# Adding up half of the first unit's modulation on TensorE in the opening of a hybrid attention and pooling block

## The chip, the cores and the metric

The kernel runs on one core of a Trainium2 chip. The metric is the device time of one execution in microseconds (us); the kernel before took 1557.66 us, the median of three runs.

## The reference

One decoder layer over 256 tokens of width 4096, all in f32, with a conditioning vector c of length 4096. Cut to what matters here:

```python
c_act = jax.nn.silu(c)
mod = c_act @ w_ada[l] + b_ada[l]                 # (1,4096) @ (4096, 12288)
shift, scale, gate = jnp.split(mod, 3, axis=-1)
h = rmsnorm(x, norm_gain[l])
h = h * (1.0 + scale[:, None, :]) + shift[:, None, :]
proj = jnp.einsum('bsd,dn->bsn', h, w_in[l])      # (256,4096) @ (4096,12288)
...                                               # attention, pooling, gating give y
y = y @ w_out[l]
x = x + gate[:, None, :] * y
return rmsnorm(x, final_gain)
```

The large product needs h, h needs shift and scale, and these are a vector times a 4096 x 8192 matrix, which has to be read from memory first.

## The kernel before, in words

**Units.** The 4096 rows of h are handled in 16 units of 256 rows, two blocks of 128 each. Unit u needs columns 256u to 256u+255 of the shift part and of the scale part of w_ada, 512 columns over all 32 row blocks. `ada_tasks` (line 174) makes 16 tasks for a unit. Each fetches two row blocks, here called a pair, into one `raw` tile of 512 KB by two transfers (line 193), and hands the adding up to `late_work`, which holds it back by one task. So the first unit has pairs 0 to 15. The adding up, `ada_acc` (line 153), is one VectorE instruction for each row block: the accumulator plus the block times its column of `cact` (silu of c, spread over the 128 partitions). For the first unit the accumulator is the SBUF tile `aflat`, for later ones a PSUM tile.

**build_h** (line 201) closes a unit: TensorE transposes the accumulator in four pieces (line 210), VectorE sums over the 128 rows (line 212, `pc`), three small VectorE operations make shift and scale columns (lines 216 to 218), ScalarE applies them to the transposed x (line 226, `hf`) and rounds (line 228, `hh`), and VectorE takes the remainder (line 229, `hl`).

**The opening.** All 16 tasks of the first unit are issued before anything else, `A0 = 1` unit, with the column constants (line 131) put in after the fourth task and the eight loads of x after the fifth. ScalarE squares x with a running sum (line 325), lines 147 to 151 make the reciprocal root, VectorE makes two diagonal tiles `diag_r` from it (line 330), and TensorE multiplies x by them in f32 (line 338), which transposes and scales it: here called the flips, in sixteen groups of four, of which twelve stand ahead of the first unit's transposes and four behind. ScalarE copies each group out (line 342).

**The visits.** After that the kernel goes over 24 chunks of 512 columns of w_in again and again, each time with the units that are ready. A piece of w_in (two row blocks by 512 columns) is fetched into a `raw` tile (line 236), rounded on ScalarE (`wh`, line 242), its remainder taken on VectorE (`wl`, line 243), and multiplied in three products on TensorE (line 253). The adding up of the next unit runs beside it at a fixed rate.

**What sets the order.** Each engine works off its instructions in the order in which the built program has them. All transfers are issued on SP in order. There are seven `raw` tiles in turn, for pairs of w_ada and pieces of w_in alike, so each transfer into one waits until the tile seven places earlier has been read. Four PSUM tiles `psm` serve flips, transposes and later accumulators.

```python
RAWB = 7
...
    todo.insert(EARLY, load_columns)
...
                for q in range(NFLIP):
                    flip_x(q)
    for u in range(A0):
        build_h(u, first[u][0][0], hp, xT)
    for q in range(NFLIP, 8):
        flip_x(q)
```

Of the kernel before, what the change touches and what calls it, by code (L numbers as in the profile page):

```python
# [7 lines left out]
F32 = mybir.dt.float32  # L8
F32R = mybir.dt.float32r
AF = mybir.ActivationFunctionType  # L10
ALU = mybir.AluOpType
AX = mybir.AxisListType

P = 128
S = 256
NT = S // P
D = 4096
KT = D // P
CH = 512
# [11 lines left out]
A0 = 1  # L31
# [24 lines left out]
def tile_hybrid_block(  # L56
# [17 lines left out]
    nc = tc.nc  # L74
# [4 lines left out]
    strm = ctx.enter_context(tc.tile_pool(name="strm", bufs=2))  # L79
# [8 lines left out]
    ps_m = ctx.enter_context(tc.tile_pool(name="ps_m", bufs=PSMB, space=PSUM))  # L88

    def misc():  # L90
        return ps_m.tile([P, CH], F32, name="psm")

    def raw_tile():
        return strm.tile([P, RAW], F32, name="raw", bufs=RAWB)
# [11 lines left out]
    cact = const.tile([P, KT], F32, name="cact")  # L106
# [46 lines left out]
    def ada_acc(acc, rt, kts, width, init=None):  # L153
        for i, kt in enumerate(kts):
            r = rt[:, i * width:(i + 1) * width]
            if kt == 0 and init is None:
                nc.vector.tensor_scalar(out=acc, in0=r, scalar1=cact[:, 0:1], scalar2=None, op0=ALU.mult)
            else:
                nc.vector.scalar_tensor_tensor(out=acc, in0=r, scalar=cact[:, kt:kt + 1],  # L159
                                               in1=init if kt == 0 else acc,  # L160
                                               op0=ALU.mult, op1=ALU.add)
# [3 lines left out]
    def late_work(f, lag=None):  # L165
        delayed.append(f)
        while len(delayed) > (HOLD if lag is None else lag):
            delayed.pop(0)()

    def flush_work():  # L170
        while delayed:
            delayed.pop(0)()

    def ada_tasks(u, pool):
        w = 2 * UNITS[u] * P
        n = RAW // w
        cs = slice(US[u] * P, US[u + 1] * P)
        acc = []
        tasks = []
        for a in range(0, KT, n):  # L180
            kts = list(range(a, min(KT, a + n)))

            def f(kts=kts):
                if not acc:
                    acc.append((adap.tile([P, 2 * HB * P], F32, name="aflat") if u < A0 else misc())[:, 0:w])
                rt = raw_tile()
                m = len(kts)
                v = rt[:, 0:m * w].rearrange("p (n s d) -> p n s d", n=m, s=2)
                if m == 1:
                    nc.sync.dma_start(out=v[:, 0], in_=wa_v[:, kts[0], 0:2, cs])  # L190
                else:
                    for i in range(2):
                        nc.sync.dma_start(out=v[:, :, i], in_=wa_v[:, kts[0]:kts[-1] + 1, i, cs])
                late_work(lambda: ada_acc(acc[0], rt, kts, w))
            tasks.append(f)
        return acc, tasks

# [3 lines left out]
    def build_h(u, acc, pool, xT):  # L201
        flush_work()
        uk, k0 = UNITS[u], US[u]
        if u >= A0:
            flat = adap.tile([P, 2 * HB * P], F32, name="aflat")
            nc.scalar.copy(out=flat[:, 0:2 * uk * P], in_=acc)
            acc = flat
        pt = misc()
        for j in range(2 * uk):
            nc.tensor.transpose(out=pt[:, j * P:(j + 1) * P], in_=acc[:, j * P:(j + 1) * P], identity=ident)  # L210
        pc = const.tile([P, 2 * HB], F32, name="pc", bufs=2)
        nc.vector.tensor_reduce(out=pc[:, 0:2 * uk], in_=pt[:, 0:2 * uk * P].rearrange("p (j d) -> p j d", d=P),
                                axis=AX.X, op=ALU.add)
        s12 = const.tile([P, 2, HB], F32, name="s12", bufs=2)
        ks = slice(k0, k0 + uk)
        nc.vector.tensor_tensor(out=s12[:, 0, 0:uk], in0=pc[:, 0:uk], in1=colB[:, ks], op=ALU.add)
        nc.vector.tensor_tensor(out=s12[:, 1, 0:uk], in0=pc[:, uk:2 * uk], in1=gainc[:, ks], op=ALU.mult)
        nc.vector.tensor_tensor(out=s12[:, 1, 0:uk], in0=s12[:, 1, 0:uk], in1=gb[:, ks], op=ALU.add)  # L218
        for a in range(0, uk, 2):
            kk = k0 + a  # L220
            if kk % HB == 0:
                htile[kk // HB] = [pool.tile([P, HB, S], F32R, name=n, align_bytes=LINE) for n in ("hh", "hl")]
            hh, hl = [v[:, kk % HB:kk % HB + 2] for v in htile[kk // HB]]
            hf = strm.tile([P, 2, S], F32, name="hf")
            for i in range(2):
                nc.scalar.activation(out=hf[:, i], in_=xT[:, kk + i], func=AF.Identity,  # L226
                                     scale=s12[:, 1, a + i:a + i + 1], bias=s12[:, 0, a + i:a + i + 1])
            nc.scalar.copy(out=hh, in_=hf)
            nc.vector.tensor_tensor(out=hl, in0=hf, in1=hh.bitcast(F32), op=ALU.subtract)  # L229
            for i in range(2):  # L230
                hs[kk + i] = (hh[:, i], hl[:, i])
# [81 lines left out]
    done = [0] * NCH  # L313
    used = [0] * NCH
    first = [ada_tasks(u, adap) for u in range(A0)]
    todo = [f for _, t in first for f in t]
    xs = []
# [36 lines left out]
# [5 lines that stand above are left out]
    state = {"ready": A0, "built": A0, "cur": ada_tasks(A0, adap), "credit": 0.0, "age": 0}  # L359

    def ada_hook(n):
        st = state
        st["credit"] += n * RATES[min(st["built"], len(RATES) - 1)]
        st["age"] += 1
        while st["cur"] and st["cur"][1] and st["credit"] > 0:
            if len(st["cur"][1]) == 1 and min(used) < ((US[st["built"] + 1] - 1) // HB - WIN + 1) * HB:
                st["credit"] = 0.0
                break
            st["cur"][1].pop(0)()
            st["credit"] -= ADA_COST  # L370
        if st["cur"] and not st["cur"][1]:
            u = st["built"]
            build_h(u, st["cur"][0][0], hp, xT)
            st["built"] += 1
            st["age"] = 0
            st["cur"] = ada_tasks(u + 1, adap) if u + 1 < NU else None
        if st["age"] >= LAG:
            st["ready"] = st["built"]
# [219 lines left out]
    for c, ch in enumerate(order):  # L598
# [5 lines left out]
        elif 12 <= ch < 16:  # L604
            i = ch - 12
# [145 lines left out]
```

## Time and profile before

| | |
|---|---|
| three runs | 1555.61, 1557.66, 1560.14 us; median 1557.66 |
| the profiled execution | 1554.48 us, of which span 1552.7 us |
| TensorE (PE) | 1504.9 us busy, 97% of the span |
| VectorE (DVE) | 1393.0 us, 90% |
| ScalarE (ACT) | 822.9 us, 53% |
| GpSimd (POOL) | 384.3 us, 25% |
| transfers | 491.15 MB, mean 316 GB/s |

The span is the time from the first to the last instruction of the execution that the profiler took; 1.78 us lie around it. A busy share says how long an engine had something in work, not that it set the pace. All times in rows are us from the start of the span unless marked ns.

### The profile page before, as it was taken

To read this page: it belongs to the slowest core of one execution; us is meant where nothing else is said; L and a number is where in the kernel's file an instruction comes from. 1 tells how busy PE (TensorE), PEld (TensorE's weight loads), DVE (VectorE), ACT (ScalarE), POOL (GpSimd) and SP (SyncE) were. 2 spreads that over 40 slices of the span, in tenths; PEclk is the share of its full clock that TensorE was granted. 3 is DMA by queue.
4 is the path that set the end of the run, shared out by engine and by line. 5 is a ranking of instruction groups with operands and counts; after the bars stand their busy time and mean duration, and the time that the engine had idled before them with its cause. 6 is when DMAs were issued, how large, how long until landed. Compare 5 with 4: busy or idle time off the path is not lost.

```text
span 1552.7 us, 20698 instructions
## 1 busy us (share of the span) xinstructions
PE 1504.9 (97%) x6979; PEld 1247.7 (80%) x6979; DVE 1393.0 (90%) x1666; ACT 822.9 (53%) x1075; POOL 384.3 (25%) x235
## 2 busy tenths in 40 slices
PE   3999999999999999999999999999999999999997
PEld 2777788888888888888888888888898878888875
DVE  5999999999989889898899998999988889888886
ACT  5666555555555655555555554556554434444434
POOL 0001545555454545545453431000000000000000
PEclk9999999999999999999999999999999999999999
DMA  9999999999999899999999999886777999999986
GB/s 334 356 355 369 313 332 309 346 299 348 332 300 347 297 342 307 321 350 324 330 349 309 335 344 327 286 268 208 247 240 259 307 346 346 340 330 324 325 307 245
DMA packets 324091, 491.15 MB, mean 316 GB/s; under 512 B 19320, under 2 KB 150664, under 8 KB 323984
## 3 DMA queue, kind: packets, MB, share of 16 engines
q1 hardware_dynamic: 323984, 489.82, 92.8%
q8 instruction: 55, 0.90, 0.2%
q14 instruction: 52, 0.43, 0.1%
HBM read 485.55 MB, written 4.19 MB: 315 GB/s over the span
## 4 chain that ended last, share of the span: by engine, by line
PE 88%; DMA 5%; DVE 4%; issue 1%; ACT 1%; SPq 0%; DVEq 0%; ACTq 0%
PE mm L253 82%; DMA raw<-in_w_ada_dram 3%; DVE wl L243 1%; DVE aflat L159 1%; PE psm L628 1%; PE psm L253 1%; DVE gacc L159 1%; DMA raw<-in_w_out_dram 1%; DMA sb<-in_x_dram 0%; PE psm L210 0%; PE psm L421 0%; PE psm L445 0%; DMA raw<-in_w_in_dram 0%; PE psm L534 0%; PE psm L533 0%
## 5 line engine op out<-in xcount | busy, mean ns | idle before, releaser
L242 ACT CAST wh<-raw 128x1024 fp32r<-128x1024 f32 x514 | 537.5, 1051 | 546.1 <-PE mm L253 408.1
L243 DVE TENSOR_TENSOR wl<-raw,wh 128x1024 fp32r<-128x1024 f32 x514 | 715.0, 1396 | 56.7 <-ACT wh L242 53.5
L253 PE MATMUL mm<-wh,hh 128*128 128x512 f32 x1536 | 603.8, 393 | 4.1 <-ACT wh L242 3.3
L253 PE MATMUL mm<-wh,hl 128*128 128x512 f32 x1536 | 599.8, 391 | 0.2 <-DVE hl L229 0.2
L253 PE MATMUL mm<-wl,hh 128*128 128x512 f32 x1536 | 414.8, 391 | 0.0
L159 DVE SCALAR_TENSOR_TENSOR psm<-raw,cact,psm 128x512 f32<-128x512 f32 x465 | 349.3, 751 | 18.5 <-DMA raw<-in_w_ada_dram 11.9
L299 POOL TENSOR_TENSOR sa<-part,sa 128x512 f32<-128x512 f32 x150 | 250.3, 1690 | 410.7 <-ACT part L298 410.7
L253 PEld LDWEIGHTS mm<-wh,hh 128*128 128x128 f32 x1536 | 288.5, 188 | 65.9 <-ACT wh L242 6.7
L253 PEld LDWEIGHTS mm<-wl,hh 128*128 128x128 f32 x1536 | 287.2, 188 | 61.0 <-DVE wl L243 1.8
L253 PEld LDWEIGHTS mm<-wh,hl 128*128 128x128 f32 x1536 | 288.6, 188 | 58.8 <-DVE hl L229 0.5
L253 PE MATMUL mm<-wh,sa 128*128 128x512 f32 x896 | 221.6, 389 | 0.0
L159 DVE SCALAR_TENSOR_TENSOR gacc<-raw,cact,gacc 128x512 f32<-128x512 f32 x248 | 185.8, 749 | 23.7 <-DMA raw<-in_w_ada_dram 19.5
L253 PEld LDWEIGHTS mm<-wh,sa 128*128 128x128 f32 x896 | 168.0, 188 | 34.8
L299 POOL TENSOR_TENSOR sb<-part,sb 128x512 f32<-128x512 f32 x80 | 133.2, 1687 | 151.9 <-ACT part L298 151.9
L298 ACT COPY part<-mm 128x512 f32<-128x512 f32 x230 | 124.0, 589 | 29.7 <-PE mm L253 29.7
L253 PE MATMUL mm<-wl,sa 128*128 128x512 f32 x448 | 120.0, 390 | 1.3 <-DVE wl L243 1.2
L253 PEld LDWEIGHTS mm<-wl,sa 128*128 128x128 f32 x448 | 83.9, 188 | 19.5 <-DVE wl L243 2.1
L338 PE MATMUL psm<-diag_r,sb 128*128 128x128 f32 x128 | 16.2, 292 | 15.9 <-DMA raw<-in_w_ada_dram 15.9
L159 DVE SCALAR_TENSOR_TENSOR aflat<-raw,cact,aflat 128x512 f32<-128x512 f32 x31 | 23.3, 752 | 8.4 <-DMA raw<-in_w_ada_dram 7.5
L338 PEld LDWEIGHTS psm<-diag_r,sb 128*128 128x128 f32 x128 | 16.0, 208 | 16.0 <-DVE diag_r L330 16.0
L294 ACT COPY sa<-mm 128x1024 f32<-128x1024 f32 x16 | 16.3, 1017 | 13.1 <-PE mm L253 13.0
L226 ACT ACTIVATE hf<-xT,s 128x256 f32<-128x256 f32 x32 | 17.5, 596 | 10.3 <-DVE s L218 10.3
(124 smaller groups left out, 709.4 us busy)
## 6 DMA issues: line engine op xcount, KB each, us to landing
raw<-in_w_in_dram SPq DMA_DIRECT2D x384, 512.0 KB, 5.7
raw<-in_w_ada_dram SPq DMA_DIRECT2D x512, 256.0 KB, 5.4
raw<-in_w_ada_dram SPq DMA_DIRECT2D x128, 512.0 KB, 5.9
raw<-in_w_out_dram SPq DMA_DIRECT2D x128, 512.0 KB, 6.3
sb<-in_x_dram SPq DMA_DIRECT2D x16, 512.0 KB, 5.7
raw<-in_w_pool_dram SPq DMA_DIRECT2D x8, 512.0 KB, 4.3
out_dram<-sb SPq DMA_DIRECT2D x16, 256.0 KB, 2.6
fg<-in_final_gain_dram SPq DMA_DIRECT2D x8, 256.0 KB, 4.8
```

The source lines that it names most:

```text
L159: nc.vector.scalar_tensor_tensor(out=acc, in0=r, scalar=cact[:, kt:kt + 1], in1=init if kt == 0 else acc, op0=ALU.mult, op1=ALU.add)
L226: nc.scalar.activation(out=hf[:, i], in_=xT[:, kk + i], func=AF.Identity, scale=s12[:, 1, a + i:a + i + 1], bias=s12[:, 0, a + i:a + i + 1])
L242: nc.scalar.copy(out=wh[:, 0:n], in_=v[:, 0:n])
L243: nc.vector.tensor_tensor(out=wl[:, 0:n], in0=v[:, 0:n], in1=wh[:, 0:n].bitcast(F32), op=ALU.subtract)
L253: nc.tensor.matmul(pt[t], lhsT=hv[i][p][:, t * P:(t + 1) * P], rhs=w[:, i], start=started, stop=ended)
L294: nc.scalar.copy(out=accs[ch], in_=pt)
L298: nc.scalar.copy(out=part, in_=pt[:, t])
L299: nc.gpsimd.tensor_tensor(out=accs[ch][:, t], in0=part, in1=accs[ch][:, t], op=ALU.add)
L338: nc.tensor.matmul(px[:, i * S + t * P:i * S + (t + 1) * P], lhsT=xs[q][:, t, (2 * a + i) * P:(2 * a + i + 1) * P], rhs=diag_r[:, t], star ...
L628: nc.tensor.matmul(pt[t], lhsT=h[:, t * P:(t + 1) * P], rhs=w, start=False, stop=last and e == len(seq) - 1)
```

## The change

For the first unit alone, the even row block of each pair is added up on VectorE as before, and the odd one by a TensorE matmul with one column of `cact` as stationary tile and the 512 columns of the block as moving data, into one row of a PSUM tile `row` that is kept over the whole opening. build_h copies that row to SBUF on ScalarE and adds it on VectorE to the first row of `aflat`, ahead of the transposes.

```diff
+    row = ps_m.tile([P, CH], F32, name="psm")
+
+    def row_acc(rt, kts, width):
+        for i, kt in enumerate(kts):
+            r = rt[:, i * width:(i + 1) * width]
+            if kt % 2 == 0:
+                ada_acc(first[0][0][0], rt, kts[:1], width)
+            else:
+                nc.tensor.matmul(row[0:1, 0:width], lhsT=cact[:, kt:kt + 1], rhs=r, start=(kt == 1), stop=(kt == KT - 1))
...
-                late_work(lambda: ada_acc(acc[0], rt, kts, w))
+                if u < A0:
+                    late_work(lambda: row_acc(rt, kts, w))
+                else:
+                    late_work(lambda: ada_acc(acc[0], rt, kts, w))
...
+        if u < A0:
+            line = strm.tile([P, 2, S], F32, name="hf").rearrange("p a s -> p (a s)")
+            nc.scalar.copy(out=line[0:1], in_=row[0:1])
+            nc.vector.tensor_tensor(out=acc[0:1], in0=acc[0:1], in1=line[0:1], op=ALU.add)
```

Lines after these stand 10 to 17 lines lower in the changed kernel (the flips at 355, the matmuls of the visits at 270, the row matmuls at 182).

On TensorE, the end of the twelfth flip group and the first unit's transposes, before:

```order
L338 MATMUL psm<-diag_r,sb 128x128 [waits DMAHW4_49,Activation_49]
L338 MATMUL psm<-diag_r,sb 128x128 x3
L338 MATMUL psm<-diag_r,sb 128x128 [waits Activation_49]
L338 MATMUL psm<-diag_r,sb 128x128 x3
L210 MATMUL psm<-ident,aflat 128x128 [waits DVE_49,Activation_49]
L210 MATMUL psm<-ident,aflat 128x128 x3
```

The same place now, where lines 355 and 227 are the flips and the transposes:

```order
L355 MATMUL psm<-diag_r,sb 128x128 [waits Activation_49]
L355 MATMUL psm<-diag_r,sb 128x128 x3
L182 MATMUL psm<-raw,cact 1x512 [waits DMAHW4_49,DMAHW3_49]
L182 MATMUL psm<-raw,cact 1x512 [waits DMAHW6_49,DMAHW5_49]
L182 MATMUL psm<-raw,cact 1x512 [waits DMAHW7_49,DMAHW0_49]
L182 MATMUL psm<-raw,cact 1x512 [waits DMAHW2_49,DMAHW1_49]
L182 MATMUL psm<-raw,cact 1x512 [waits DMAHW4_49,DMAHW3_49]
L182 MATMUL psm<-raw,cact 1x512 [waits DMAHW6_49,DMAHW5_49]
L182 MATMUL psm<-raw,cact 1x512 [waits DMAHW7_49,DMAHW0_49]
L182 MATMUL psm<-raw,cact 1x512 [waits DMAHW2_49,DMAHW1_49]
L182 MATMUL psm<-raw,cact 1x512 [waits DMAHW4_49,DMAHW3_49]
L227 MATMUL psm<-ident,aflat 128x128 [waits DVE_49]
```

Of the 16 row matmuls, those of pairs 0 to 6 stand ahead of the flips and the nine of pairs 7 to 15 between the twelve flip groups and the transposes.

On SP, the transfers of pairs 13 (`raw_299`), 14 (`raw_304`) and 15 (`raw_309`), of the first piece of w_in (`raw_362`), of the next unit's first two pairs and of the second piece of w_in, now:

```order
L203 DMA raw_299<-in_w_ada_dram 128x2x256 [waits DMAHW7_49,DVE_49,PE_49]
L203 DMA raw_299<-in_w_ada_dram 128x2x256 [waits DMAHW0_49]
L203 DMA raw_304<-in_w_ada_dram 128x2x256 [waits DMAHW1_49,DVE_49,PE_49]
L203 DMA raw_304<-in_w_ada_dram 128x2x256 [waits DMAHW2_49]
L203 DMA raw_309<-in_w_ada_dram 128x2x256 [waits DMAHW3_49,DVE_49,PE_49]
L203 DMA raw_309<-in_w_ada_dram 128x2x256 [waits DMAHW4_49]
L253 DMA raw_362<-in_w_in_dram 128x2x512 [waits DMAHW5_49,DVE_49,PE_49]
L203 DMA raw_381<-in_w_ada_dram 128x2x256 [waits DMAHW6_49,DVE_49,PE_49]
L203 DMA raw_381<-in_w_ada_dram 128x2x256 [waits DMAHW7_49]
L203 DMA raw_384<-in_w_ada_dram 128x2x256 [waits DMAHW0_49,DVE_49,PE_49]
L203 DMA raw_384<-in_w_ada_dram 128x2x256 [waits DMAHW1_49]
L253 DMA raw_392<-in_w_in_dram 128x2x512 [waits DMAHW2_49,DVE_49,PE_49]
```

The order of the transfers is the same as before; what is new is the wait for TensorE beside the one for VectorE. Pair 14 takes the tile of pair 7, pair 15 that of pair 8, and the first piece of w_in that of pair 9.

On ScalarE, from the twelve flip copies to the rounding of h, now (259 is the rounding of a w_in piece, 223 the copy of the row, 243 and 245 make `hf` and `hh`):

```order
L359 COPY xT<-psm 128x512 [waits PE_49] x12
L259 CAST wh<-raw 128x1024 [waits DMAHW5_49]
L223 COPY hf<-psm 1x512 [waits PE_49,Activation_49]
L359 COPY xT<-psm 128x512 [waits PE_49]
L243 ACTIVATE hf<-xT,s_326 128x256 [waits DVE_49,Activation_49]
L243 ACTIVATE hf<-xT,s_326 128x256
L359 COPY xT<-psm 128x512 [waits PE_49]
L245 CAST hh<-hf 128x512 [waits Activation_49]
```

The new copy of the row stands behind the rounding of the first w_in piece. VectorE has its instructions in the like order: the remainder of that piece, then the add of the row, then the sum over the transposes. From the second unit on, the order of all engines is that of before but for a few early places of ScalarE and VectorE.

## Rows read from the trace of the kernel before

**Rows 1.** The page, chain that ended last, share by engine.

```profile
PE 88%; DMA 5%; DVE 4%; issue 1%; ACT 1%; SPq 0%; DVEq 0%; ACTq 0%
```

**Rows 2.** Busy time by stage: PE, PEld, DVE, ACT, POOL, granted clock, DMA share, GB/s.

```profile
300.00:600.00 300.00, 300.00 (x1335) 248.39 (x1334) 275.68 (x282) 170.31 (x222) 156.53 (x93) 1.00 0.96 321
```

**Rows 3.** Timeline of VectorE, opening: start, length, operation, count, idle before and releaser.

```profile
9.48 3.20 DVE L159 SCALAR_TENSOR_TENSOR aflat<-raw,cact,aflat 128x512 f32<-128x512 f32 x4 [0.24 <-DMA raw<-in_w_ada_dram]
...
24.70 2.33 DVE L159 SCALAR_TENSOR_TENSOR aflat<-raw,cact,aflat 128x512 f32<-128x512 f32 x3
...
27.07 0.75 DVE L159 SCALAR_TENSOR_TENSOR aflat<-raw,cact,aflat 128x512 f32<-128x512 f32 x1
27.73 0.48 DVE L330 TENSOR_SCALAR diag_r<-ident,rr 128x128 f32<-128x128 f32 x2
28.13 14.13 DVE L159 SCALAR_TENSOR_TENSOR aflat<-raw,cact,aflat 128x512 f32<-128x512 f32 x18
...
43.68 1.22 DVE L243 TENSOR_TENSOR wl<-raw,wh 128x1024 fp32r<-128x1024 f32 x1
```

**Rows 4.** Timeline of TensorE, opening.

```profile
11.49 0.42 PE L137 MATMUL psm<-ident,rows 112*128 112x112 f32 x1 [7.92 <-DMA rows<-in_pool_scale_dram]
...
28.07 12.50 PE L338 MATMUL psm<-diag_r,sb 128*128 128x128 f32 x96 [15.86 <-DMA raw<-in_w_ada_dram]
42.41 0.63 PE L210 MATMUL psm<-ident,aflat 128*128 128x128 f32 x4 [1.84 <-DVE aflat L159]
42.87 3.74 PE L338 MATMUL psm<-diag_r,sb 128*128 128x128 f32 x32
47.47 0.50 PE L253 MATMUL mm<-wh,hh 128*128 128x512 f32 x1 [0.87 <-ACT hh L228]
```

**Rows 5.** Timeline of ScalarE, opening.

```profile
12.49 0.63 ACT L325 ACTIVATE hf<-sb 128x512 f32<-128x512 f32 x1 [0.29 <-DMA sb<-in_x_dram]
...
20.48 0.63 ACT L325 ACTIVATE hf<-sb 128x512 f32<-128x512 f32 x1 [1.33 <-DMA sb<-in_x_dram]
...
32.56 0.59 ACT L342 COPY xT<-psm 128x512 f32<-128x512 f32 x1 [0.31 <-PE psm L338]
...
41.09 1.05 ACT L242 CAST wh<-raw 128x1024 fp32r<-128x1024 f32 x1
```

**Rows 6.** Timeline of the SP queue: issues of transfers in the opening.

```profile
1.65 4.01 SPq L193 DMA_DIRECT2D raw<-in_w_ada_dram  x8
...
15.19 18.70 SPq L193 DMA_DIRECT2D raw<-in_w_ada_dram  x22
34.32 0.37 SPq L236 DMA_DIRECT2D raw<-in_w_in_dram  x1
```

**Rows 7.** The page, DMA issues: count, size, median us from issue to landing.

```profile
raw<-in_w_in_dram SPq DMA_DIRECT2D x384, 512.0 KB, 5.7
```

**Rows 8.** Groups by line and shape: count, busy us, mean ns, idle before.

```profile
L342 ACT COPY xT<-psm 128x512 f32<-128x512 f32 x16 | 9.4, 586 | 10.4 <-PE psm L338 10.4
L229 DVE TENSOR_TENSOR hl<-hf,hh 128x512 fp32r<-128x512 f32 x16 | 11.8, 739 | 1.8 <-ACT hh L228 1.8
```

**Rows 9.** The chain in order of time: the first long run of the visits.

```profile
48.20 30.01 PE mm L253 x131
```

**Rows 10.** Busy time by stage, with the granted clock third from the end.

```profile
28.00:30.00 2.00, 1.93 (x9) 1.93 (x10) 1.93 (x5) 0.00 (x0) 0.00 (x0) 1.00 1.10 351
...
1542.00:1546.00 4.00, 0.00 (x0) 0.00 (x0) 2.84 (x9) 2.13 (x5) 0.00 (x0) 1.00 1.04 399
1546.00:1547.00 1.00, 0.00 (x0) 0.00 (x0) 1.00 (x3) 0.74 (x2) 0.00 (x0) 0.89 0.88 338
```

**Rows 11.** Waits of TensorE from 47 to 145 us: total, times, longest.

```profile
PE mm L253 <- ACT wh L242: 3.3, 4, 2.0
```

**Rows 12.** Timeline of ScalarE at 78 us, where the longest of these waits lies.

```profile
78.23 1.01 ACT L294 COPY sb<-mm 128x1024 f32<-128x1024 f32 x1 [1.70 <-PE mm L253]
79.14 2.00 ACT L242 CAST wh<-raw 128x1024 fp32r<-128x1024 f32 x2
```

## The prediction

> **What bounds the kernel now.** I read the chain that ended last first: 88% of it is TensorE [rows 1], and between 300 and 600 us TensorE is busy without a gap [rows 2]. Once the visits run, the end is their start plus a fixed amount of matmul work, so a change in the opening counts by what it does to the first visit matmul, at 47.47 us [rows 4], after which 131 matmuls follow without a break from 48.20 on [rows 9]. Next I read the opening engine by engine. Its last stretch belongs to VectorE: 18 row blocks in one piece from 28.13 to 42.26 [rows 3], then TensorE's transposes at 42.41, after 1.84 us of waiting for `aflat` [rows 4]. TensorE itself has the flips from 28.07 to 40.57 and four flip groups more behind the transposes, 3.74 us [rows 4]. SP is well ahead: the transfers of pairs 5 to 15, 22 of them, are all issued by 33.89 and the first piece of w_in at 34.32 [rows 6].
>
> **The change part by part, from the span's start.**
>
> VectorE loses 16 row blocks at 0.75 us, 12 us of work. That is worth something only if the sum is then complete earlier, and the order says that it is not: nine of the 16 row matmuls stand on TensorE behind the twelve flip groups.
>
> Start and end of the flips. They wait for `diag_r`. Before, VectorE did three row blocks from 24.70 (2.33 us), the reciprocal, one more row block, and then `diag_r` at 27.73 [rows 3]. Now it does two row blocks there and none after the reciprocal: about 1.2 us less, so the flips start at about 26.9 instead of 28.07. A flip group costs 0.59 of copy plus 0.31 of ScalarE waiting for TensorE, 0.90 us [rows 5]; twelve make 10.8, but they took 12.5, so 1.7 us are a slow start after a long idle stretch [rows 4]. Now the row matmuls of pairs 4 to 6 run just ahead of them and may take that slow start away, or not: end at 37.7 or 39.4. Nothing tells which; I take the middle, 38.5, against 40.57 before.
>
> The row matmuls. The rows have no f32 matmul with 512 columns and one stationary column. The nearest is a flip group, f32 as well, four times 128 columns: 0.90 us. A visit matmul, 512 columns in the rounded type, follows the last one after 0.23 us (131 in 30.01) [rows 9], which is the lower end; twice 0.90, as in the slow start, is the upper. I take 0.9, since type and column count are the same. Nine behind the flips make 8.1 us: 38.5 to 46.6 if their data are there.
>
> The early seven cost nothing if ScalarE's squares cover them. Those of pairs 0 to 3 push the transposes of line 137, at 11.49 before [rows 4], back by about 1.4 us at the slow rate (pair 3 was used from about 11.0 on, two blocks after 9.48 [rows 3], plus 1.8). The squares, which began at 12.49, then begin near 13.8. They had 1.33 us of waiting for x before 20.48 [rows 5], which takes it up; without that cover it would be 1.3 us more. The `row` tile holds one of four PSUM tiles, so the flips turn over in three; ScalarE is 0.31 us ahead in each group, so that costs nothing either.
>
> The transfers. This is the part that hangs on SP. Pair 14 needs the `raw` tile of pair 7, which TensorE now reads after the flips, at 38.5 + 0.9 = 39.4. So SP stops behind pair 13, and queued behind it are pairs 14 and 15, the first w_in piece and the next unit's pairs. Pair 14 goes out at 39.4, pair 15 at 40.3, w_in at 41.2, where before it went out at 34.32. When does that piece land? By the median from issue to landing, 5.7 us [rows 7], at 46.9. By the start of the program, the other place where the queue starts empty: first issue at 1.65 [rows 6], third tile used at 9.48 as it landed [rows 3], 7.8 us later, so 47.2. By bandwidth alone, three tiles of 0.52 MB at 351 GB/s [rows 10], 4.5 us, at 43.9: the lower end. I take 47.1.
>
> From there to the transposes. ScalarE rounds the piece, 1.05 [rows 5], to 48.2. Only then, in its order, comes the copy of `row`, 0.59 like a flip copy [rows 8], since 512 elements of one partition take as long as of 128 at best; it lies beside VectorE's remainder, 1.22 [rows 3], to 49.4. The add of the row is priced as `hl`, 0.74 [rows 8], to 50.2. Transposes at 50.3 instead of 42.41, 7.9 us late. If the piece landed at 43.9, the nine row matmuls would bind instead: 46.6, copy to 47.2, add to 48.0, 5.6 us late.
>
> From the transposes to the first visit matmul. Before, 5.06 us [rows 4], with the remainder of the piece in the middle of VectorE's chain, which is now ahead of it. TensorE still has 4.2 us of transposes and flips to do, and ScalarE two flip copies between, so I take 4.6: first visit matmul at 54.9 instead of 47.47, 7.4 us late.
>
> Sum: 7.4 us on the profiled execution's own 1554.48 makes 1561.9; that execution was 3.2 us under the median of the runs, 1557.66, so the median comes to 1565.1. All 16 units behind it keep their order, and TensorE has hardly a gap to lend.
>
> **The rivals.**
>
> *Lent back later (not slower).* While TensorE waits, up to seven `raw` tiles land, so the visits start with more in hand than before. If TensorE's waits for rounded pieces between 47 and 145 us, 3.3 us [rows 11], come from late transfers, they go: 7.4 - 3.3 = 4.1, at 1561.8. The point from which it decides is 2.7 us given back, since 0.3% of the time, about what a measurement of this kernel can tell from no change, is 4.7 us. Against it: in the longest, ScalarE's rounding at 79.14 stood behind a copy that waited 1.70 us for TensorE's own matmuls [rows 12]. That is order, and the order there is kept.
>
> *Half clock behind the wait.* TensorE idles from the last row matmul, 46.6, to the transposes, 3.7 us. If it comes back slow, as at the first flips, 1.7 us are added: 9.1, at 1566.8. For it: the slow start of the flips, though the granted clock reads 1.00 (2.4 GHz) from 28 to 30 us. Against: at the end of the program it idles from 1542 on and is granted 1.00 for four more microseconds, and 0.89 on average in the next one [rows 10], so it fell only after more than 3.7 us, and the 1.84 us before the old transposes left no mark. The Trainium skill ("TensorE: Matmul & The Clock Gate", Part 1) says that the array's clock is low by default and that idling sends it back; by that rule this rival holds if the idle stretch is long enough, which no row here settles for 3.7 us.
>
> *The meant effect (not slower).* If TensorE took each row matmul when its pair had landed, past the waiting flips, VectorE's half would end with the transfers: last issue 33.89, landing some 5.7 later at 39.6, last block 0.75, copy 0.59, add 0.74, transposes at 41.7 instead of 42.41: 0.7 us faster, 1557.0, no change to tell. It decides if TensorE's order is no order. The only view with a word on it is the order of instructions, and there each wait stands in one row of matmuls. The Trainium skill (the same page, Part 3, "What overlaps and what doesn't") says that matmuls start and end strictly in program order, and only weight loads are pulled ahead; by that rule this rival falls and the 7.9 us stand. The trace agrees as far as it goes: the flips behind the old transposes did not start until these did, at 42.87, though `diag_r` and x had been there since 28.
>
> **How the numbers follow.** Forecast 0.61, with its own range from 1562.5 (flips end at 37.7, early landing) to 1568 (39.4, late landing, and scatter of the runs, 2.3 us either way). Lent back 0.13; half clock 0.13; meant effect 0.06; something that I don't see 0.07. The predicted time is the forecast's, 1565. For 8 in 10 the range reaches from the lent-back case to the half clock one with some scatter: 1560.5 to 1569. Slower by over 0.3%: nearly all of forecast and half clock, 0.71. Within 0.3%: lent back, meant effect, and what of the forecast's scatter falls under 1562.3, 0.22. Faster: 0.07, of the unseen and the scatter of the meant effect.
>
> **What would show it.** Right: nine row matmuls directly behind the twelfth flip group; SP issuing nothing between about 31 and 39 us, with the DMA share of a window from 37 to 41 us far under the 1.10 of 28 to 30 us [rows 10]; the first rounding on ScalarE near 47, transposes near 50, the first visit matmul near 55; the span longer by about as much as that matmul is later. Wrong in a term: flips that end outside 37.7 to 39.4, row matmuls at 0.25 or 1.8 us each, or a w_in piece landing well before 46. Wrong in the mechanism: row matmuls between flip groups, pair 14 issued before the flips end, or a late first visit with a span that has not grown, with the waits of [rows 11] gone.

## The result, and the profile after

The changed kernel took 1565.99 us (median of four runs, 1564.49 to 1566.19) beside 1557.26 us for the kernel before in the same session: 8.7 us slower, ratio 1.0064 with a 95% interval of 1.0052 to 1.0076. The ratio on record is not the quotient of the two medians, which is 1.0056; taken by itself it would put the loss at 10.0 us. In a later session it took 1563.93 beside 1555.60, 8.3 us slower, ratio 1.0055 (1.0041 to 1.0068).

TensorE's timeline of the changed kernel (start, length, operation, count, idle before it and what ended that), the rows that answer to [rows 4]; a row matmul leaves two records:

```profile
25.53 3.57 PE L182 MATMUL psm<-raw,cact 128*1 128x512 f32 x4 [3.39 <-DMA raw<-in_w_ada_dram]
29.03 11.87 PE L355 MATMUL psm<-diag_r,sb 128*128 128x128 f32 x96
40.83 7.03 PE L182 MATMUL psm<-raw,cact 128*1 128x512 f32 x16
48.90 1.02 PE L182 MATMUL psm<-raw,cact 128*1 128x512 f32 x2 [1.04 <-DMA raw<-in_w_ada_dram]
53.15 1.12 PE L227 MATMUL psm<-ident,aflat 128*128 128x128 f32 x4 [3.23 <-DVE aflat L224]
54.06 5.72 PE L355 MATMUL psm<-diag_r,sb 128*128 128x128 f32 x32
59.54 0.48 PE L270 MATMUL mm<-wh,hh 128*128 128x512 f32 x1
```

Nine row matmuls stand directly behind the twelve flip groups, eight in 7.03 us, 0.88 each. The transposes come 10.7 us later than before, the first visit matmul 12.1. The last four flip groups take 5.72 us where they took 3.74.

SP's queue and then ScalarE in the same stretch, as in [rows 6] and [rows 5]:

```profile
16.20 27.59 SPq L203 DMA_DIRECT2D raw<-in_w_ada_dram  x22
43.90 0.40 SPq L253 DMA_DIRECT2D raw<-in_w_in_dram  x1
```

```profile
50.20 1.04 ACT L259 CAST wh<-raw 128x1024 fp32r<-128x1024 f32 x1 [8.68 <-DMA raw<-in_w_in_dram]
51.15 0.57 ACT L223 COPY hf<-psm 1x512 f32<-1x512 f32 x1
```

The 22 issues of pairs 5 to 15 now take until 43.79, and the first piece of w_in goes out at 43.90 instead of 34.32. Busy time by stage (stretch, length, TensorE's busy time and count, granted clock, DMA share, GB/s) shows the hole:

```profile
32.00:37.00 5.00, 5.00 (x47) 1.00 0.80 256
37.00:41.00 4.00, 4.00 (x36) 1.00 0.01 4
41.00:45.00 4.00, 4.00 (x10) 1.00 0.46 140
...
50.00:55.00 5.00, 1.85 (x9) 0.64 1.08 373
55.00:60.00 5.00, 5.00 (x31) 0.68 0.92 298
```

From 37 to 41 us next to nothing is transferred, 4 GB/s. And after the 3.23 us of waiting for `aflat` the granted clock is 0.64 and 0.68 of 2.4 GHz, so the transposes and the late flips ran in good part at 1.2 GHz.

How far the delay reaches is read off the chain in order of time. The changed kernel:

```profile
59.78 30.27 PE mm L270 x132
92.08 10.75 PE mm L270 x39
...
211.47 68.06 PE mm L270 x300
...
1305.22 59.85 PE mm L270 x264
```

and the kernel before, three rows that were not shown yet:

```profile
80.24 9.14 PE mm L253 x39
...
197.54 68.06 PE mm L253 x300
...
1292.23 59.85 PE mm L253 x264
```

The unbroken run of 300 visit matmuls begins 13.9 us later, and the run of 264 near the end still 13.0 later; at the end of the span 11.6 are left (1564.3 beside 1552.7 us). So the delay comes about before 200 us, and I use the start of that run of 300 as the mark for each kernel below. From the mark to the run of 264 all fourteen profiles need 1093.5 to 1096.5 us, and from the mark to the end of the span 1352.1 to 1356.5, so the mark of one profile tells its time to within some 4 us and not better.

### The profile page after: what moved, and what is told of

Its sections match the earlier page's. It is cut to its first block, busy times and chain, and to the rows that moved or that the text cites. A ratio compares the mean times of both kernels' runs of the same rounds, so it can differ in the third digit from the quotient of the medians.

```text
span 1564.3 us, 20754 instructions
## 1 busy us (share of the span) xinstructions
PE 1528.0 (98%) x7011; PEld 1253.1 (80%) x7011; DVE 1381.9 (88%) x1651; ACT 822.5 (53%) x1076; POOL 384.7 (25%) x235
## 4 chain that ended last, share of the span: by engine, by line
PE 93%; DMA 3%; DVE 2%; ACT 1%; issue 1%; SPq 0%; DVEq 0%; ACTq 0%
PE mm L270 84%; DMA raw<-in_w_ada_dram 1%; PE psm L355 1%; PE psm L645 1%; PE psm L270 1%; DMA raw<-in_w_in_dram 1%; DVE wl L260 1%; PE psm L551 0%; PE psm L550 0%; PE psm L227 0%; PE psm L549 0%; DMA sb<-in_x_dram 0%; PE psm L438 0%; PE psm L462 0%; DMA raw<-in_w_out_dram 0%
## 5 line engine op out<-in xcount | busy, mean ns | idle before, releaser
L182 PE MATMUL psm<-raw,cact 128*1 128x512 f32 x32 | 20.6, 791 | 13.5 <-DMA raw<-in_w_ada_dram 13.5
L159 DVE SCALAR_TENSOR_TENSOR aflat<-raw,cact,aflat 128x512 f32<-128x512 f32 x15 | 11.3, 751 | 24.7 <-DMA raw<-in_w_ada_dram 24.6
```

What stands on the lines that cost most here:

```text
L182: nc.tensor.matmul(row[0:1, 0:width], lhsT=cact[:, kt:kt + 1], rhs=r, start=(kt == 1), stop=(kt == KT - 1))
```

## The experiments

Twelve kernels ran in three sessions; before stood at 1555.45, 1555.83 and 1555.60 us in them. "Visits" is the start of the first visit matmul, "ready" the number of w_in pieces that ScalarE had rounded by then, "mark" the start of the run of 300, each of one profiled execution.

| kernel | visits | ready | mark | median us | ratio to before (95%) |
|---|---|---|---|---|---|
| before | 47.47 | 1 | 197.54 | 1557.26 | 1 |
| changed | 59.54 | 1 | 211.47 | 1565.99 | 1.0064 (1.0052 to 1.0076) |
| changed, again | 56.32 | 1 | 208.63 | 1563.93 | 1.0055 (1.0041 to 1.0068) |
| sixteen tiles | 55.10 | 3 | 201.15 | 1555.71 | 1.0003 (0.9994 to 1.0012) |
| before with sixteen tiles | 47.77 | 1 | 199.82 | 1556.05 | 1.0007 (0.9997 to 1.0017) |
| flips between | 58.27 | 3 | 204.98 | 1560.42 | 1.0036 (1.0023 to 1.0049) |
| kept busy | 56.02 | 2 | 204.54 | 1561.23 | 1.0044 (1.0031 to 1.0058) |
| stop alone | 56.98 | 1 | 207.67 | 1562.59 | 1.0042 (1.0028 to 1.0056) |
| early seven alone | 47.80 | 1 | 199.85 | 1556.25 | 1.0003 (0.9994 to 1.0011) |
| late nine alone | 59.22 | 1 | 209.72 | 1565.95 | 1.0075 (1.0057 to 1.0093) |
| sixteen tiles, flips between | 58.34 | 3 | 205.27 | 1560.52 | 1.0030 (1.0019 to 1.0040) |
| changed, padded | 59.24 | 1 | 209.54 | 1564.13 | 1.0057 (1.0045 to 1.0070) |
| before, padded by 128 bytes | 47.69 | 1 | 196.89 | 1553.40 | 0.9984 (0.9975 to 0.9993) |
| before, padded by 256 bytes | 48.46 | 1 | 198.61 | 1555.64 | 1.0001 (0.9992 to 1.0009) |

**Theories.** Mine: the nine late row matmuls hold `raw` tiles behind the flips, SP stops, and the pieces and the last pairs land late. First rival: the nine matmuls are simply too much work ahead of the transposes. Second: half clock after the wait.

**Sixteen tiles.** The first unit's pairs lie in the sixteen `sa` tiles, which nothing else uses yet, so no transfer waits for a row matmul.

```diff
-                rt = raw_tile()
+                rt = slot_a([P, RAW]) if u < A0 else raw_tile()
```

> The changed kernel, but the first unit's 16 pairs go into the 16 SBUF tiles that later hold the visits' sums, so that no transfer has to wait for a tile that TensorE still has to read. Theory 'held tiles and row matmuls': transfers do not stop between 37 and 41 us; the first w_in piece lands near 41 instead of 50.2; the nine row matmuls, 40.9 to 48.9 us, now bind by themselves; copy and add after them put the transposes at about 50.4 instead of 53.15; the idle stretch is too short to lose the clock, so the flips behind take 3.7 instead of 5.7; first visit matmul near 55 instead of 59.5, about 4.5 us faster than the changed kernel, some 4 us (0.3%) slower than before. Rival 'held tiles alone': back to the time of before, 1557. Rival 'matmul price alone': no change, 1566.

The same edit in the kernel before is the control:

> Control: the kernel before with the same 16 tiles for the first unit's pairs. All theories: VectorE bounds the opening up to 42.3 us and its tiles came free in time, so first visit matmul at 47 to 48 us and the time of before within 1 us. If held tiles bounded before as well, up to 2.5 us faster.

Measured: no difference from before in either, where I had expected some 4 us to stay in the changed kernel. TensorE's timeline of the changed kernel with sixteen tiles, and its waits from 44 to 150 us for rounded pieces (total, times, longest):

```profile
40.38 7.89 PE L182 MATMUL psm<-sa,cact 128*1 128x512 f32 x18
50.00 0.66 PE L227 MATMUL psm<-ident,aflat 128*128 128x128 f32 x4 [1.73 <-DVE aflat L224]
50.49 3.74 PE L355 MATMUL psm<-diag_r,sb 128*128 128x128 f32 x32
55.10 0.74 PE L270 MATMUL mm<-wh,hh 128*128 128x512 f32 x2 [0.87 <-ACT hh L245]
```

```profile
PE mm L270 <- ACT wh L259: 0.6, 2, 0.3
```

So the loss is gone, but not because the sum is early: the row matmuls still end at 48.3 and the visits still begin 7.3 us after the control's. At the mark 1.3 us of that are left. The first w_in piece went out at 34.10, ScalarE had rounded three pieces by the first visit matmul, and the waits for rounded pieces, 3.3 us before [rows 11], shrank to 0.6. This is the rival "Lent back later", and it takes place where the pieces are there. That it is the pieces alone isn't shown: in the kernels with three ready the built order of ScalarE also has three roundings ahead of `hh`, in the changed kernel one. Over the table, the stretch from the first visit matmul to the mark is 149.2 to 152.3 us in the kernels with one piece ready, 148.5 with two, and 146.1 to 146.9 with three.

**Stop alone.** VectorE adds up everything, as before; TensorE only reads the tiles of pairs 7 to 13 behind the flips. All seven, since the pool hands out whichever tile is to come free first.

```diff
+        row = ps_m.tile([P, CH], F32, name="psm") if u < A0 else None
...
+                if u < A0 and 14 <= kts[0] < 28:
+                    late_work(lambda: nc.tensor.matmul(row[0:1, 0:P], lhsT=cact[:, 0:1], rhs=rt[:, 0:P],
+                                                       start=True, stop=True))
```

> VectorE adds up all row blocks, as in the kernel before. Behind the twelve flip groups TensorE only reads the tiles of pairs 7 to 13, with seven small matmuls of 128 columns (about 0.2 us each) whose result nobody uses. So the transfers of pairs 14 and 15 and of w_in stop as in the changed kernel, but nothing of the sum is on TensorE. If the stop of the transfers is the cause: pair 14 out near 41, w_in near 42, 7 to 8 us later than before, and the time 7 to 9 us over before, ratio 1.0045 to 1.006. If the row matmuls, the copy and the add on the way to the transposes are the cause: within 2 us of before.

Measured: 6.8 us over before. TensorE's timeline:

```profile
28.33 13.84 PE L342 MATMUL psm<-diag_r,sb 128*128 128x128 f32 x96 [16.22 <-DMA raw<-in_w_ada_dram]
42.10 1.69 PE L197 MATMUL psm<-raw,cact 128*1 128x128 f32 x14
51.02 1.09 PE L214 MATMUL psm<-ident,aflat 128*128 128x128 f32 x4 [7.23 <-DVE aflat L159]
51.90 5.14 PE L342 MATMUL psm<-diag_r,sb 128*128 128x128 f32 x32
```

With 1.69 us of work on TensorE in place of 7.9, no row to copy and none to add, the transposes are as late as in the two profiles of the changed kernel (50.71 and 53.15): TensorE waits 7.23 us for VectorE, whose last pairs have not landed. The flips ended at 42.1 here, so the first w_in piece goes out at 44.52, later than I had put it. So the stop alone brings most of the loss, 6.8 of 8.3 to 8.7 us. The ratio, 1.0042, lies a little under the 1.0045 that I had put as the least for the whole loss, and its interval overlaps those of the changed kernel, so the runs don't tell whether the row matmuls add anything to the stop.

**Halves of the row matmuls.** Blocks that are not in ON_PE go to VectorE; range(1, 14, 2) is the early half, range(15, KT, 2) the late one.

```diff
...
+            elif kt not in ON_PE:
+                acc = first[0][0][0]
+                nc.vector.scalar_tensor_tensor(out=acc, in0=r, scalar=cact[:, kt:kt + 1], in1=acc,
+                                               op0=ALU.mult, op1=ALU.add)
...
```

> Only the row matmuls of pairs 0 to 6, ahead of the flips, are left on TensorE; VectorE does both blocks of pairs 7 to 15. If the stop of the transfers is the cause, which these seven cannot bring about: same as before, ratio 0.999 to 1.001, w_in out near 34. If the flips that end later because of them (2.4 us in the changed kernel against the forecast) or the copy and the add cost by themselves: 2 to 4 us over before, ratio 1.0015 to 1.0025.

> Only the nine row matmuls of pairs 7 to 15, behind the flips, are left on TensorE; VectorE does both blocks of pairs 0 to 6. Stop of the transfers as in the changed kernel, pair 14 out 0.5 to 1 us earlier than there (41 to 41.5). If the stop is the cause: nearly all of the loss stays, ratio 1.005 to 1.0065. If the early seven carry a part of it: that part is gone, ratio under 1.0045.

Measured: the early seven cost nothing (0.4 us, inside the interval), the late nine the whole loss (10.1 us). First w_in piece on SP's queue and transposes on TensorE, with the early seven alone:

```profile
34.36 0.37 SPq L258 DMA_DIRECT2D raw<-in_w_in_dram  x1
```

```profile
42.72 0.63 PE L232 MATMUL psm<-ident,aflat 128*128 128x128 f32 x4 [2.49 <-DVE aflat L229]
```

and with the late nine alone:

```profile
44.89 0.40 SPq L258 DMA_DIRECT2D raw<-in_w_in_dram  x1
```

```profile
53.74 1.12 PE L232 MATMUL psm<-ident,aflat 128*128 128x128 f32 x4 [3.22 <-DVE aflat L229]
```

The row's copy and add are in both, so they cost nothing where the pieces are in time. The late nine came out above my 1.0065: the flips end 1.0 us later than in the changed kernel's first profile, pair 14 goes out at 42.88 and not at 41 to 41.5, and two of the six runs took 1570.7 and 1571.4 us.

**Flips between.** One flip group stands between the row matmuls of two pairs, so the tiles come free earlier.

```diff
...
-                for q in range(NFLIP):
-                    flip_x(q)
+                flips += [(q, a) for q in range(NFLIP) for a in range(2)]
+        if flips:
+            q, a = flips.pop(0)
+            flip_x(q, (a,))
...
```

> The changed kernel with the twelve flip groups ahead of the transposes issued one for each task, so that each of the nine late row matmuls stands between flip groups instead of behind all of them. Theory 'held tiles and row matmuls': tiles come free as pairs land, TensorE works through 10.8 us of flips and 8 us of row matmuls from about 29 on without a break to 48, transposes near 50.3, first visit matmul near 55, about 4.5 us faster than the changed kernel, like the run with 16 tiles. Rival 'matmul price alone': 1566. Rival 'order alone' (no matmul price): transposes near 43, 1557 to 1558.

Measured: 5.0 us over before, some three fifths of the loss. The first piece of w_in goes out at 37.10, but the last row matmul ends at 49.29 and the visits start at 58.27, not near 55: the transposes come at 51.81 behind 2.52 us of idling, and the late flips take 5.36.

With sixteen tiles as well:

> The first unit's 16 pairs lie in sixteen tiles that are free then, so no transfer stops, and one flip group stands between two pairs' row matmuls, so the sum is complete earlier than with the sixteen tiles alone (transposes near 46 instead of 50). If only the transfers count: same as before, ratio 0.999 to 1.001, no better than the sixteen tiles alone. If the lateness of the transposes still costs something there: up to 3 us less than the sixteen tiles alone.

A miss: 4.7 us over before, worse than sixteen tiles alone, though no transfer waits for a row matmul. Its TensorE has no gap from 28.0 to 49.1 us: four flip groups in 3.84, eight times a row matmul and a flip group in 2.04, and a last row matmul. So the transposes did not come at 46, as I had thought, but here:

```profile
51.62 0.85 PE L227 MATMUL psm<-ident,aflat 128*128 128x128 f32 x4 [2.52 <-DVE aflat L224]
52.26 5.21 PE L355 MATMUL psm<-diag_r,sb 128*128 128x128 f32 x32
```

Behind 2.52 us of idling the late flips run at the low clock (0.69 granted from 50 to 55 us) and the visits begin 3.2 us later than with sixteen tiles alone: 1.6 are there at the transposes already, and the late flips add 1.5. So the first rival holds to a part: with the flips between, the last row matmul ends later still (49.1 beside 48.3), and what is lent back, 4 to 6 us by the profile one takes for before, covers only so much of a late start.

**Kept busy.** Fourteen matmuls that nobody reads fill TensorE's idle stretch ahead of the transposes.

```diff
+            spin = misc()
+            for j in range(14):
+                nc.tensor.matmul(spin[:, (j % 4) * P:(j % 4 + 1) * P], lhsT=ident, rhs=ident, start=True, stop=True)
```

> The changed kernel with 14 f32 matmuls of 128 by 128 on the identity put between the last row matmul and the transposes (their result is read by nobody), about 3.1 us, which fills TensorE's wait from 49.9 to 53.15. Theory 'clock lost in the wait': granted clock 1.00 in 50 to 55 us instead of 0.64, the four flip groups behind take 3.7 instead of 5.7, first visit matmul near 57.6, 2 us faster than the changed kernel. Rival 'the late flips are slow for another reason': same time as the changed kernel or some tenths more.

```profile
47.52 3.39 PE L224 MATMUL psm<-ident 128*128 128x128 f32 x28
51.54 0.66 PE L230 MATMUL psm<-ident,aflat 128*128 128x128 f32 x4 [0.63 <-DVE aflat L227]
52.03 3.74 PE L358 MATMUL psm<-diag_r,sb 128*128 128x128 f32 x32
```

The late flips are back at 3.74 us, with 1.00 granted from 50 to 55 us where the changed kernel has 0.64, so the 2.0 us were the clock's. The timing (5.8 us over before) is under that of the changed kernel, but the intervals overlap: the runs show the mechanism, not its price in the total.

**The changed kernel again, and the padding.** The windows of the sixteen-tile kernels showed the same transfers at 384 GB/s that run at 348 into the `raw` tiles. In the built program the `raw` tiles start 384 bytes past a multiple of 512 in each partition, the `sa` tiles at one. A pool ahead of `strm` moves them by 128 bytes:

```diff
+    padp = ctx.enter_context(tc.tile_pool(name="padp", bufs=1))
+    padp.tile([P, 32], F32, name="pad")
     strm = ctx.enter_context(tc.tile_pool(name="strm", bufs=2))
```

> The changed kernel itself, once more beside the others. 1.005 to 1.0075 of before, as its first timing gave; the transfers stop again between the issue of pair 13 and the end of the flips, and the run of 252 visit matmuls that started at 152.5 starts between 150 and 153.

> The changed kernel with 128 bytes of padding ahead of the pool of the seven raw tiles, so that each starts at a multiple of 512 bytes in its partition and not 128 bytes short of one. If the destination's place is why the transfers of pairs ran at 384 GB/s into the sixteen tiles and at 348 into these: 380 GB/s or more from 28 to 32 us. The stop stays, since it is a matter of order; w_in lands at most 1 us earlier, so the time is 1.004 to 1.0065 of before. If the stop were only a lack of transfer rate, the loss would mostly go.

> The kernel before with the same padding. If the transfers up to about 140 us set the pace of the opening and of the first visits, and the destination's place costs them a tenth of their rate: 380 GB/s or more from 28 to 41 us, less waiting for rounded pieces between 47 and 145 us (3.3 us before), and the time 1 to 5 us under before, ratio 0.997 to 0.9993. If the place does nothing, or something else sets the pace: same as before, 0.9995 to 1.0005.

> The kernel before with 256 bytes of padding in that place, so that the raw tiles start 128 bytes past a multiple of 512: the control of the kernel with 128 bytes. If it is the multiple of 512 that counts: 348 GB/s from 28 to 37 us as before, and the same time, ratio 0.9993 to 1.001. If any other place does it: as fast as with 128 bytes.

Measured from 28 to 37 us (stretch, length, granted clock, DMA share, GB/s), first the kernel before with 128 bytes:

```profile
28.00:37.00 9.00, 1.00 1.09 383
```

and then with 256:

```profile
28.00:37.00 9.00, 1.00 1.10 348
```

The rate follows the place. For the changed kernel it does not help, as the stop is one of order. The kernel before with 128 bytes is the one version that beats both: 1553.40 beside 1555.60 us, 2.2 us. Its waits for rounded pieces fell only from 3.3 to 2.7 us, as they did with 256 bytes, and its visits begin no earlier. So where the 2.2 us come from is not shown.

The changed kernel's second profile stands beside its first below.

## Why the prediction was right

The forecast was 1565.0; the medians are 1565.99 and 1563.93. TensorE's timeline in the second profile of the changed kernel:

```profile
27.45 11.25 PE L355 MATMUL psm<-diag_r,sb 128*128 128x128 f32 x96
38.62 8.14 PE L182 MATMUL psm<-raw,cact 128*1 128x512 f32 x18
50.71 0.66 PE L227 MATMUL psm<-ident,aflat 128*128 128x128 f32 x4 [3.94 <-DVE aflat L224]
51.20 5.37 PE L355 MATMUL psm<-diag_r,sb 128*128 128x128 f32 x32
56.32 0.47 PE L270 MATMUL mm<-wh,hh 128*128 128x512 f32 x1
```

- **Start and end of the flips**, forecast 38.5, from 37.7 to 39.4. 38.7 here, 40.9 in the first profile, outside the range. The squares wait for the last x tiles, and their landing moves from execution to execution: the sum over the squares (line 147) ran at 25.45 in the one and 23.86 in the other. What the term lacked: the row matmuls of pairs 5 and 6 ran at 1.2 GHz (1.78 us each in the first profile, 0.50 granted from 20 to 28 us) and stood ahead of the flips, which began 0.6 us after `diag_r` was ready, in both profiles. In return the slow start of the flips shrank: 11.9 and 11.3 us for twelve groups, 12.5 before.
- **Row matmuls**, forecast 0.9: 0.88.
- **Stop of the transfers**: as forecast, pair 14 out 1.0 us after the flips' end (41.88), w_in 2.0 us later. In the second profile w_in goes out at 41.69 (forecast 41.2).
- **Landing**, forecast 5.9 us from issue: 6.3 in the first profile, 6.1 in the second, where the rounding starts at 47.76 (forecast 48.2 for its end, measured 48.8).
- **Rounding, copy, remainder, add**: forecast 3.2 us from the landing to the transposes, 3.0 measured, and transposes at 50.71 where 50.3 stood.
- **From the transposes to the first visit matmul**, forecast 4.6: 5.6 and 6.4. This step was wrong. "Half clock behind the wait", which I priced at 1.7 and gave 0.13, took place in both profiles: the late flips took 1.6 and 2.0 us longer. What misled me was the end of the program, where the clock fell only after more than 3.7 us of idling [rows 10]; here 3.23 were enough. The Trainium skill ("TensorE: Matmul & The Clock Gate", Part 1) has the array fall back to the low clock when it idles; the trace agrees, 0.64 granted from 50 to 55 us.
- **Lent back later**: it did not happen. TensorE's waits for rounded pieces stayed at 2.9 and 3.3 us against 3.3 [rows 11]. The forecast's reason, order, is not refuted; the sixteen tiles add that pieces in hand and roundings ahead together do give back 4 to 6 us.
- **The meant effect**: nothing could be gained here. Where no transfer stops and VectorE is relieved of seven blocks, the transposes start at 42.72 against 42.41.
- **The sum.** Forecast 7.4 us; the timings say 8.7 and 8.3, the marks of the two profiles 13.9 and 11.1. The profiled executions are single ones: that of before took 1554.48 us, 2.8 under the 1557.26 of its session, and the changed kernel's 1566.09, 11.6 more. So of the 13.9 us at the first mark, 2.3 are gone again at the end, 2.8 come from a profiled execution of before that was shorter than its median, and 8.8 are left, as the medians say. The second profile is of an execution of 1566.88 us, 2.9 over its own median. That the mark of before, 197.54, is early shows in the three other kernels whose time is that of before and whose visits start as early: they have it at 198.61 to 199.85. In both marks of the changed kernel 1.6 us are the run of 39 matmuls, 10.75 us instead of 9.14, at a low clock once more. What takes the 2.3 us back behind the mark stays open.

So the mechanism was right, and two sizes were off: the late flips by 1.6 to 2.0 us, and in the first profile the end of the flips by 2.4. The first visit came 12.1 and 8.9 us late where 7.4 stood. By its mechanism the rival "Half clock behind the wait" took place on top of the forecast, and by size the losses, 8.7 and 8.3 us, lie nearer its 9.1 than the forecast's 7.4, the second only just; I had given it 0.13 beside 0.61. That the number came out within 1 us is in part luck.

## What to carry to other kernels

An engine that takes over reading a buffer also takes over when the buffer comes free. Before moving work, look where the new reader stands in its engine's order and count how many buffers it holds behind the work ahead of it; if that is all of them, as it was here, the queue of transfers stops, whatever else is gained. A late start is partly given back where the data behind it are ready, and not where the same stop has held them up.

## What the hardware showed that I had not expected

- **Place of the destination.** Transfers of 1 KB per partition and row ran at 383 to 384 GB/s into tiles at multiples of 512 bytes and at 348 to 349 into tiles 128 bytes off such a multiple on either side, a tenth less, with the DMA engines as busy (1.09 and 1.10). The runs don't tell 512 from 256, since both places tried are off either. The Trainium skill ("DMA: Bandwidth & Descriptors", "How a descriptor splits into AXI transactions") says that a descriptor that does not start at a multiple of 256 bytes has its first transaction start at the boundary below, and that the bytes fetched for nothing still cost beats on the bus; it says so of reading, and here it is the place written to that changed. So the reason is not shown.
- **The clock after short waits.** In the opening, TensorE's late flips kept 3.74 us after waits from 0.50 to 2.49 us (the latter with the early seven alone) and took 4.6 to 6.2 us after those from 2.52 us (sixteen tiles, flips between) to 7.23. Nor is a wait's length all there is to it: the same wait of 2.05 us for a rounded piece, near 80 to 92 us, was followed by the low clock in some profiles and not in others. In the changed kernel (stretch, length, TensorE's busy time, granted clock, DMA share, GB/s):

```profile
88.00:92.00 4.00, 2.04 (x9) 1.00 1.08 364
92.00:96.00 4.00, 3.92 (x10) 0.57 1.07 370
```

and in the kernel with the late nine alone, after the same wait:

```profile
88.00:92.00 4.00, 1.95 (x10) 1.00 1.08 366
92.00:96.00 4.00, 4.00 (x18) 1.00 1.07 367
```
